# Strassen's seven quarter products for the mixing gates and merge gates of a hybrid layer

## The chip, the cores and the metric

The kernel runs on one core of a Trainium2 chip. The metric is device time in microseconds (us) of one execution. TensorE is called PE in the profile (PEld is its weight load), VectorE DVE, ScalarE ACT, GpSimd POOL and SyncE SP; SP issues nearly all DMAs.

## The reference

One decoder layer on 512 tokens of 1024 channels. The input is normalised, multiplied by one wide matrix `w_in` (1024 x 12288) and cut into pieces: `q_a, k_a, v_a, z_a` for attention, `x_m, z_m, o_m` for an mLSTM branch, and `gates`.

```python
xn = rmsnorm(h, norm_in_g[layer])
proj = xn @ w_in[layer]
q_a, k_a, v_a, z_a, x_m, z_m, o_m, gates = jnp.split(proj, SPLIT_POINTS, axis=-1)
...
y_a = (y_a * jax.nn.silu(z_a)) @ w_pa[layer]
y_m = mlstm_branch(x_m, z_m, o_m, ...) @ w_pb[layer]     # ends with h * jax.nn.silu(z_m)
g = jax.nn.sigmoid(gates.astype(jnp.float32) + gate_b[layer])
g_a, g_m = jnp.split(g, 2, axis=-1)
merged = g_a * y_a + g_m * y_m
h = h + (merged @ w_out[layer]).astype(h.dtype)
```

`z_m` has 2048 columns (the mixing gates) and `gates` has 2048 (the merge gates). Only these two projections change.

## The kernel before, in words

**Tiling.** `w_in` lies in DRAM as 96 chunks of 128 output columns, each a 128 x 1024 tile (eight blocks of 128 input channels side by side). The normalised, transposed input is held as eight pairs `xh[k]`, `xl[k]` of 128 x 512 tiles: a value is split into a rounded part (h) and the rest (l), and a product is three matmuls, h·h, h·l and l·h (`mm3`). A chunk is fetched (`fetch`, tile `raw`), split into `whi` on ACT and `wlo` on DVE (`halves`, `weights`), and multiplied by `proj_t`: 8 blocks x 3 matmuls of 512 columns into one PSUM bank. There are four buffers each of `raw`, `whi` and `wlo` (`NRAW`, `NHL`), two PSUM banks with the tag mm and six with the tag x.

**Stages.** First the sixteen `x_m` chunks with the convolution (tile `conv`), the folded q-k products (`kp`) and the S sums; this is called the xm stretch here. The S sums of a head lie in a wide tile `sraw`. Then four heads (`head`): the matmuls `num` (256 or 258 columns), their statistics on DVE, four `zm` chunks with SiLU (`silu2`), transposes `hT`, the next head's values `v` and output gate `om`, and the product `ym` with `w_pb`, summed in `ymacc`. Then eight pairs of attention heads (`qa`, `ka`, `za`, `sa`, `pT`, `pv`). Then the sixteen `gate` chunks (eight for the attention branch, tiles `thg`, and eight for the mLSTM branch, applied to `ymacc`), the product `ya` with `w_pa`, and the output projection.

**What sets the order.** All operations are recorded first. `Recorder.issue` then walks a model of the engines and gives each engine a fixed order: the ready operation of the smallest number goes first, and weights are numbered 300 earlier (`AHEAD`) so that they run ahead of their matmuls. On the chip each engine runs its list strictly in that order. Buffers come from pools of fixed size (`NSLOT` small tiles of 516 columns, `NWIDE` and `NWT` wide ones), and an operation that needs a buffer waits until one is free. Since a helper records everything, nearly all instructions carry line 333 in the profile, and one goes by the names of tiles.

Of the kernel before, what the change touches and what calls it, by code (L numbers as in the profile page):

```python
# [11 lines left out]
F32 = mybir.dt.float32  # L12
# [5 lines left out]
P = 128  # L18
T = 512
# [318 lines left out]
def hybrid_layer(ctx, tc, a, out):  # L338
# [43 lines left out]
    def mm3(ps, lh, ll, rh, rl, first, last):  # L382
        PE.matmul(ps, lh, rh, start=first, stop=False)
        PE.matmul(ps, lh, rl, start=False, stop=False)
        PE.matmul(ps, ll, rh, start=False, stop=last)
# [129 lines left out]
    for k in range(NK):  # L515
# [109 lines left out]
    def block_v(h):  # L625
# [8 lines left out]
        for s in range(NT):  # L634
# [8 lines left out]
            V.tensor_sub(v2[:, :512], ps, v1[:, :512].bitcast(F32))  # L643
            v_of[h].append((v1, v2))

    gps = pv_bank("gates")
    sps = None
    waiting = []
    sraw = []
    for ct in range(NMT):  # L650
        h, c = divmod(ct, 4)
        ps = early_ps[ct] if ct < EARLY else proj_t(CXM + ct, "xm")
        if c == 0:
            Mh, Ml = fold_qk(h)
# [19 lines left out]
        kf = slot("kf")[:, :P]  # L674
        A.activation(kf, ps[:, T - P:], AF.Copy)
        if ct == 0:
            fold_gates()
        waiting.append((ct, m, xc))
        if c == 3:

            R.together()
            for ct_, m_, xc_ in waiting:
                for i, (w, x) in enumerate(((1, m_[:, 3:259]), (1, m_[:, 259:515]), (0, xc_[:, :256]), (0, xc_[:, 256:]))):
                    PE.matmul(gps[32 * i:32 * i + 32, :256], ust[w][:, ct_, :], x, start=ct_ == 0, stop=ct_ == NMT - 1,
                              tile_position=(0, 32 * i))
# [79 lines left out]
    def head(h):  # L765
# [209 lines left out]
    for d in range(NK):
        for g in range(2):
            ps = proj_t(CG + NK * g + d, "gate")
            th = slot("thg")[:, :T]
            A.activation(th, ps, AF.Tanh, scale=0.5, bias=hs[:, 32 + 8 * g + d:33 + 8 * g + d])
            if g == 0:  # L980
                ga.append(th)
            else:
                V.scalar_tensor_tensor(ym[d], th, 1.0, ym[d], op0=OP.add, op1=OP.mult)
# [76 lines left out]
def _bucket(dist):  # L1060
# [86 lines left out]
```

## Time and profile before

| what | value |
|---|---|
| median of 3 runs | 905.69 us (904.43 to 906.78) |
| the profiled execution | 907.21 us, span 905.2 us |
| PE busy | 886.7 us, 98% of the span |
| DVE busy | 576.0 us, 64% |
| ACT busy | 385.8 us, 43% |
| POOL busy | 71.5 us, 8% |
| DMA | 104.64 MB, mean 116 GB/s |

The span is the time between the first and the last instruction of the profiled execution; the rest of its time lies around it. A busy time is the share in which at least one instruction of the engine ran. The duration of a matmul in the profile covers its whole way through the array, and the next one starts before it ends, so the cost of a matmul is read from the distance between starts.

### The profile page before, as it was taken

The page shows a single profiled execution, that of the slowest core. Times are in us where ns is not written, and L with a number is a line of the kernel's source. Part 1 is how long each engine was busy: PE and PEld are TensorE (multiplying, and loading weights), DVE is VectorE, ACT ScalarE, POOL GpSimd, SP SyncE. Part 2 cuts the span into 40 slices and gives each one's busy share as a digit, 9 for nine tenths or more (in the row PEclk, how much of TensorE's full clock was granted, in tenths as well). Part 3 has the DMA queues.
Part 4 walks back from the last instruction along what each step waited for, and adds up shares of the span by engine and source line. Part 5 has one row for each costly group of instructions (what it writes and reads, how often), then busy time and mean ns, then how long its engine had stood idle before and what let it go on. Part 6 is the DMA issues. An engine that isn't in the chain of part 4 may idle for free.

```text
span 905.2 us, 11844 instructions
## 1 busy us (share of the span) xinstructions
PE 886.7 (98%) x4340; PEld 727.1 (80%) x4340; DVE 576.0 (64%) x1154; ACT 385.8 (43%) x724; POOL 71.5 (8%) x136
## 2 busy tenths in 40 slices
PE   7899999999999999999999999999999999999997
PEld 5577878788878888887888888888888888888886
DVE  4998987785428546744855477874777843328533
ACT  7445544443343332332333265563665543325222
POOL 0950110000000000000000111101011100000000
PEclk9799999999999999999999999999999999999999
DMA  9652334233049234204313222313223223224221
GB/s 305 223 173 99 124 118 161 82 129 105 11 152 341 102 117 163 93 23 162 126 53 124 96 73 105 128 59 104 74 79 105 71 81 101 98 94 157 77 81 59
DMA packets 38801, 104.64 MB, mean 116 GB/s; under 512 B 4308, under 2 KB 6100, under 8 KB 38744
## 3 DMA queue, kind: packets, MB, share of 16 engines
q1 hardware_dynamic: 38600, 103.63, 33.6%
q8 instruction: 34, 0.56, 0.2%
q10 hardware_dynamic: 144, 0.26, 0.1%
q14 instruction: 23, 0.19, 0.1%
HBM read 93.35 MB, written 15.77 MB: 121 GB/s over the span
## 4 chain that ended last, share of the span: by engine, by line
PE 93%; DVE 4%; issue 1%; ACT 1%; DMA 1%; SPq 0%; DVEq 0%; ACTq 0%
PE zm L333 10%; PE gate L333 10%; PE ym L333 10%; PE om L333 9%; PE xm L333 8%; PE out L333 5%; PE qa L333 5%; PE za L333 5%; PE ka L333 5%; PE va L333 5%; PE ya L333 5%; PE num L333 3%; PE S L333 3%; PE pv L333 2%; PE sa L333 2%; PE pT L333 2%
## 5 line engine op out<-in xcount | busy, mean ns | idle before, releaser
L333 DVE TENSOR_TENSOR wlo<-raw,whi 128x1024 fp32r<-128x1024 f32 (+1 forms) x126 | 151.4, 1203 | 159.7 <-ACT whi L333 159.7
L333 ACT ACTIVATE whi<-raw 128x1024 fp32r<-128x1024 f32 (+1 forms) x126 | 128.1, 1019 | 284.7 <-PE zm L333 79.2
L333 PE MATMUL xm<-xh,whi 128*128 128x512 f32 x128 | 54.3, 427 | 5.2 <-ACT whi L333 5.2
L333 PE MATMUL xm<-xl,whi 128*128 128x512 f32 x128 | 54.0, 423 | 2.1 <-DVE xl L333 2.1
L333 PE MATMUL xm<-xh,wlo 128*128 128x512 f32 x128 | 53.2, 418 | 1.7 <-DVE wlo L333 1.7
L333 PE MATMUL om<-wlo,xh 128*128 128x512 f32 x128 | 50.9, 397 | 0.0
L333 PE MATMUL gate<-xh,whi 128*128 128x512 f32 x128 | 50.9, 397 | 0.0
L333 PE MATMUL zm<-xh,whi 128*128 128x512 f32 x128 | 50.8, 397 | 0.0
L333 PE MATMUL gate<-xl,whi 128*128 128x512 f32 x128 | 50.7, 396 | 0.0
L333 PE MATMUL om<-whi,xh 128*128 128x512 f32 x128 | 50.6, 396 | 0.0
L333 PE MATMUL om<-whi,xl 128*128 128x512 f32 x128 | 50.6, 395 | 0.0
L333 PE MATMUL gate<-xh,wlo 128*128 128x512 f32 x128 | 50.6, 395 | 0.0
L333 PE MATMUL ym<-yl,whi 128*128 128x512 f32 x128 | 50.5, 394 | 0.0
L333 PE MATMUL zm<-xl,whi 128*128 128x512 f32 x128 | 50.4, 394 | 0.0
L333 PE MATMUL ym<-yh,wlo 128*128 128x512 f32 x128 | 50.4, 394 | 0.0
L333 PE MATMUL zm<-xh,wlo 128*128 128x512 f32 x128 | 50.4, 394 | 0.0
L333 PE MATMUL ym<-yh,whi 128*128 128x512 f32 x128 | 50.2, 392 | 0.0
L333 ACT ACTIVATE p<-p,mx 128x128 f32<-128x128 f32 (+1 forms) x64 | 35.4, 556 | 14.3 <-DVE mx L333 14.3
L333 DVE CUSTOM_DVE_ANT_0 p<-sa,tb 128x128 f32<-128x128 f32 (+1 forms) x64 | 28.3, 488 | 18.2 <-PE sa L333 18.2
L333 DVE SCALAR_TENSOR_TENSOR conv<-xm,half,conv 128x512 f32<-128x512 f32 x48 | 37.2, 775 | 0.8
L333 DVE TENSOR_TENSOR ymacc<-ymacc,ym 128x512 f32<-128x512 f32 x24 | 16.5, 687 | 31.2 <-PE ym L333 31.2
L333 PEld LDWEIGHTS xm<-xh,whi 128*128 128x128 f32 x128 | 25.8, 201 | 11.6 <-ACT whi L333 5.8
(253 smaller groups left out, 2222.5 us busy)
## 6 DMA issues: line engine op xcount, KB each, us to landing
raw<-in_win_dram SPq DMA_DIRECT2D x94, 512.0 KB, 3.4
raw<-in_wpb_dram SPq DMA_DIRECT2D x16, 512.0 KB, 3.2
fr<-fd SPq DMA_DIRECT2D x1, 5120.0 KB
xmd<-xm SPq DMA_DIRECT2D x16, 256.0 KB, 2.2
sxd<-sx SPq DMA_DIRECT2D x16, 256.0 KB, 2.1
xmr<-xmd SPq DMA_DIRECT2D x16, 256.0 KB, 4.2
sxr<-sxd SPq DMA_DIRECT2D x16, 256.0 KB, 4.1
tb<-fr SPq DMA_DIRECT2D x16, 256.0 KB, 3.7
```

The source lines that it names most:

```text
L333: getattr(getattr(self.nc, op.eng), fn)(*a, **k)
```

## The change

Two neighbouring chunks are taken as one product of a 256 x 1024 matrix with the 1024 x 512 input, and that is cut into quarters: halves of the 1024 input channels, halves of the 512 tokens, and the two chunks. Winograd's form of Strassen's algorithm computes the four result quarters from seven products of quarters (`pair_t`) in place of eight. Each product is four blocks x 3 matmuls of 256 columns.

- The four sums and differences of the input (t1 to t4) are made once, by `quarters`, after the twelfth `x_m` chunk: POOL scales `xt` by the gain (8 operations) and forms the differences in tiles `tq` (8 operations of 512 columns), and ACT and DVE split them into `th` and `tl`.
- The four sums and differences of a pair's weights (s1 to s4) are formed by POOL in two buffers `ws` (`NWS`), and split like a chunk. A pair takes all four `whi` and `wlo` buffers: the first chunk whole (a11, a12), s2 with s1, s3 with s4, and a22 alone (`pair_weights`).
- The seven products use three PSUM banks, `ba`, `bb` and `bd`. Some of them add onto a bank that already holds another product, and DVE or ACT reads the bank between them: p1 (ACT, from ba), p1's second half and c2 (DVE, from bb), p5 (DVE, from bd).
- `xt` and the `th`, `tl` tiles share a new pool of eight tiles of 1024 columns. To make room, `NSLOT` goes from 51 to 44, `NWIDE` and `NWT` from 4 to 2, and the S sums of each head go to DRAM (`srd`) and come back in `head`.

```diff
-        z = [silu2(proj_t(CZM + 4 * h + c, "zm"), "zm") for c in range(4)]
+        z = []
+        for c in (0, 2):
+            z += silu_pair(a["win"][CZM + 4 * h + c], a["win"][CZM + 4 * h + c + 1], "zm")
...
-    for d in range(NK):
+    for d in range(0, NK, 2):
         for g in range(2):
-            ps = proj_t(CG + NK * g + d, "gate")
+            c1, c2 = pair_t(a["win"][CG + NK * g + d], a["win"][CG + NK * g + d + 1], "gate")
...
+    def quarters():
+        for k in range(NK):
+            G.tensor_scalar(xt[k], xt[k], gain(k), None, op0=OP.mult)
...
+        for m in range(2):
+            u, w = x4[m], x4[m + 2]
+            t = [slot("tq")[:, :T].rearrange("p (k t) -> p k t", k=2) for _ in range(4)]
+            G.tensor_sub(t[0], u[:, :, late], u[:, :, early])
+            G.tensor_sub(t[1], w[:, :, late], t[0])
+            G.tensor_sub(t[2], w[:, :, late], u[:, :, late])
+            G.tensor_sub(t[3], w[:, :, early], t[1])
...
+                A.activation(h[:, cc], x, AF.Copy)
+                V.tensor_sub(l[:, cc], x, h[:, cc].bitcast(F32))
...
+    def pair_weights(src0, src1):
+
+        R.ahead = AHEAD
+        r0, r1 = fetch(src0), fetch(src1)
+        lo, hi = slice(0, 512), slice(512, 1024)
+        whole = halves(r0)
...
+        G.tensor_add(s[0], r1[:, lo], r1[:, hi])
+        G.tensor_sub(s[1], s[0], r0[:, lo])
+        t2 = two(s[1], s[0])
+        s += [tile_of(wpool, [P, 512], F32, "ws", "ws", NWS) for _ in range(2)]
+        G.tensor_sub(s[2], r0[:, lo], r1[:, lo])
+        G.tensor_sub(s[3], r0[:, hi], s[1])
+        t3 = two(s[2], s[3])
+        t4 = two(r1[:, hi], None)
...
+    def pair_t(src0, src1, name):
+
+        w = pair_weights(src0, src1)
+        t1, t2, t3, t4 = tx
+        ba, bb, bd = mm_bank(name)[:, :256], sc_bank(name)[:, :256], mm_bank(name)[:, :256]
...
+        product(ba, w["a11"], x_quarter(0, 0), True)
+        A.activation(p1[:, :256], ba, AF.Copy)
+        product(bb, w["s2"], t2, True)
+        V.tensor_add(p1[:, 256:], bb, p1[:, :256])
+        product(bd, w["s1"], t1, True)
+        V.tensor_add(p5[:, :256], bd, p1[:, :256])
+        product(ba, w["a12"], x_quarter(1, 0), False)
+        product(bb, w["s3"], t3, False)
+        V.tensor_add(c2[:, 256:], bb, p5[:, :256])
+        product(bd, w["s4"], x_quarter(1, 1), False)
+        V.tensor_add(p5[:, 256:], bd, p1[:, 256:])
+        product(bb, w["a22"], t4, False)
+        V.tensor_add(c2[:, :256], bb, p1[:, :256])
...
-            sraw.append(sr)
+            SP.dma_start(srd[h], sr)
+        if ct == 11:
+            tx = quarters()
...
-        sr = sraw[h]
+        sr = wide("sraw")
+        SP.dma_start(sr, srd[h])
...
-NSLOT = 51
+NSLOT = 44
...
-NWIDE = 4
-NWT = 4
+NWIDE = 2
+NWT = 2
+NWS = 2
```

On DVE in the gate stretch (near the end of the program), a few chunks in the middle of it read so before; `wlo` is the split of a chunk, `ymacc` and `yal` are later work:

```order
L333 TENSOR_TENSOR wlo_6919<-raw_6765,whi_6909 128x1024
L333 TENSOR_TENSOR wlo_6952<-raw_6819,whi_6942 128x1024
L333 SCALAR_TENSOR_TENSOR ymacc_2370<-thg_6949,ymacc_2370 128x512
L333 TENSOR_TENSOR yal_6965<-ya_5926,yah_6900 128x512
L333 TENSOR_TENSOR wlo_6990<-raw_6856,whi_6980 128x1024
```

After the change one pair reads so, from the split of s3 of one pair to that of s3 of the next; `gate_...` are the PSUM banks, `ws` what POOL made:

```order
L333 TENSOR_TENSOR wlo_7870<-ws_7840,whi_7857 128x512
L333 TENSOR_TENSOR wlo_7877<-raw_7642,whi_7866 128x512
L333 TENSOR_TENSOR c2_7836<-gate_7753,p1_7756 128x256
L333 SCALAR_TENSOR_TENSOR ymacc_2587<-thg_7896,ymacc_2587 128x512
L333 TENSOR_TENSOR wlo_7870<-ws_7881,whi_7857 128x512
L333 TENSOR_TENSOR p1_7888<-gate_7884,p1_7888 128x256
L333 TENSOR_TENSOR p5_7931<-gate_7910,p1_7888 128x256
L333 TENSOR_TENSOR wlo_7941<-raw_7761,whi_7928 128x1024
L333 TENSOR_TENSOR wlo_7956<-ws_7925,whi_7946 128x512
L333 TENSOR_TENSOR wlo_7956<-ws_7902,whi_7946 128x512
L333 TENSOR_TENSOR c2_7971<-gate_7884,p5_7931 128x256
L333 TENSOR_TENSOR p5_7931<-gate_7910,p1_7888 128x256
```

The splits of the next pair (7941 and twice 7956) stand between p5, which follows product 3, and c2, which follows product 5 of the running pair.

On PE, at the same place, product 7 (a22, weights 7866) follows product 6 (s4, weights 7857); 7884 is bank bb and 7910 bank bd:

```order
L333 MATMUL gate_7910<-xh_471,whi_7857 128x256
L333 MATMUL gate_7910<-xl_480,whi_7857 128x256
L333 MATMUL gate_7910<-xh_471,wlo_7870 128x256
L333 MATMUL gate_7884<-th_1400,whi_7866 128x256
L333 MATMUL gate_7884<-tl_1435,whi_7866 128x256
L333 MATMUL gate_7884<-th_1400,wlo_7877 128x256
```

Product 7 writes the bank that c2_7971 on DVE reads after product 5. Before, each chunk had a bank of its own and PE had no such order to keep.

On POOL in the xm stretch, this piece of the difference shows where the scaling of `xt` and the differences `tq` stand; `ust`, `M` and `Bv` are small preparations of the heads:

```order
-L333 TENSOR_TENSOR ust<-ust,wrep 128x16x8 x7
+L333 TENSOR_TENSOR ust<-ust,wrep 128x16x8 x5
+L333 TENSOR_SCALAR xt<-xt,pc 128x512
+L333 TENSOR_TENSOR ust<-ust,wrep 128x16x8
+L333 TENSOR_SCALAR xt<-xt,pc 128x512
+L333 TENSOR_TENSOR ust<-ust,wrep 128x16x8
+L333 TENSOR_SCALAR xt<-xt,pc 128x512 x6
 L333 TENSOR_TENSOR M<-mrow,bmask 128x512 x2
 L333 TENSOR_TENSOR Bv<-brow,bmask 128x512
```

The eight scalings stand between the last of `ust` and the preparation of the second head (`M`); the eight `tq` operations follow behind `Bv`.

## Rows read from the trace of the kernel before

**Rows 1.** The page: busy time and the chain that ended last.

```profile
PE 886.7 (98%) x4340; PEld 727.1 (80%) x4340; DVE 576.0 (64%) x1154; ACT 385.8 (43%) x724; POOL 71.5 (8%) x136
...
PE 93%; DVE 4%; issue 1%; ACT 1%; DMA 1%; SPq 0%; DVEq 0%; ACTq 0%
PE zm L333 10%; PE gate L333 10%; PE ym L333 10%; PE om L333 9%; PE xm L333 8%; PE out L333 5%; PE qa L333 5%; PE za L333 5%; PE ka L333 5%; PE va L333 5%; PE ya L333 5%; PE num L333 3%; PE S L333 3%; PE pv L333 2%; PE sa L333 2%; PE pT L333 2%
```

**Rows 2.** Chain in order of time: start, us, what.

```profile
189.79 7.14 PE num L333 x60
...
196.94 22.29 PE zm L333 x96
...
728.48 81.04 PE gate L333 x349
```

**Rows 3.** Waits of PE: total, times, longest (us).

```profile
PE kp L333 <- ACT xch L333: 2.3, 2, 1.9
```

**Rows 4.** Timeline of PE in the first head's num.

```profile
192.94 0.28 PE L333 MATMUL num<-vl,Wh 128*128 128x258 f32 x1
192.95 0.19 PEld L333 LDWEIGHTS num<-vh,Wl 128*128 128x128 f32 x1
...
193.06 0.28 PE L333 MATMUL num<-vh,Wl 128*128 128x258 f32 x1
```

**Rows 5.** Timeline of POOL: start, us, instruction.

```profile
26.84 13.06 POOL L333 TENSOR_TENSOR xt<-xt,norm 128x512 f32<-128x512 f32 x8 [0.77 <-DMA wrep<-in_wrep_dram]
...
195.94 1.05 POOL L333 TENSOR_TENSOR Bv<-brow,bmask 128x512 f32<-128x512 f32 x1 [15.15 <-PE num L333]
```

**Rows 6.** Timeline of DVE beside POOL's xt work.

```profile
26.80 1.89 DVE L333 TENSOR_TENSOR xm<-xm,norm 128x512 f32<-128x512 f32 x3 [1.66 <-ACT norm L333]
...
30.89 1.75 DVE L333 SCALAR_TENSOR_TENSOR xl<-xt,pc,xh 128x512 fp32r<-128x512 f32 x1
...
32.56 2.29 DVE L333 TENSOR_TENSOR wlo<-raw,whi 128x1024 fp32r<-128x1024 f32 x1
```

**Rows 7.** Timeline of DVE in the second head.

```profile
280.08 0.42 DVE L333 SCALAR_TENSOR_TENSOR tho<-tho,num 128x256 f32<-128x256 f32 x1 [0.28 <-PE num L333]
280.42 0.17 DVE L333 BATCH_NORM_AGGREGATE mv<-bs 128x2 f32<-128x6 f32 x1
...
283.54 1.23 DVE L333 TENSOR_TENSOR wlo<-raw,whi 128x1024 fp32r<-128x1024 f32 x1
284.68 0.16 DVE L333 TENSOR_SCALAR va<-va 128x4 f32<-128x4 f32 x1
284.75 0.68 DVE L333 SCALAR_TENSOR_TENSOR zm<-zm 128x512 f32<-128x512 f32 x1
285.35 0.16 DVE L333 TENSOR_SCALAR rh_y<-va 128x4 int32<-128x4 int32 x1
```

**Rows 8.** Groups by line and form: busy, mean ns, idle before.

```profile
L333 ACT ACTIVATE whi<-raw 128x1024 fp32r<-128x1024 f32 x118 | 125.1, 1061 | 284.3 <-PE zm L333 79.2 <-PE ym L333 57.5 <-PE gate L333 50.5
...
L333 POOL CAST ql<-ql 64x512 fp32r<-64x512 f32 x16 | 9.8, 613 | 5.8 <-DVE ql L333 5.8
```

**Rows 9.** Stretches xm, ym, num and zm, gate: length, busy PE, PEld, DVE, ACT, POOL.

```profile
60.00:170.00 110.00, 109.68 (x625) 87.59 (x624) 93.15 (x144) 52.31 (x101) 7.77 (x7) 0.99 0.36 127
327.00:349.40 22.40, 22.40 (x98) 17.87 (x96) 10.87 (x13) 5.33 (x6) 1.05 (x1) 1.00 0.49 170
349.40:379.00 29.60, 29.60 (x158) 25.27 (x158) 22.14 (x64) 9.55 (x20) 0.61 (x7) 1.00 0.39 131
728.00:809.00 81.00, 81.00 (x353) 65.58 (x352) 26.96 (x30) 26.61 (x35) 0.00 (x0) 1.00 0.28 96
```

**Rows 10.** DMA issues: count, KB, us to landing.

```profile
raw<-in_win_dram SPq DMA_DIRECT2D x94, 512.0 KB, 3.4
...
xmr<-xmd SPq DMA_DIRECT2D x16, 256.0 KB, 4.2
```

More of the change, by code (lines that the diff above doesn't have):

```diff
@@ L380, in dram, with mm3 @@
         return R.buf(lambda: dpool.tile(shape, F32, name=name), shape, F32, dram=True)
[L382 to L385, printed above, removed]
+    def mm3(ps, lh, ll, rh, rl, first, last, **kw):
+        PE.matmul(ps, lh, rh, start=first, stop=False, **kw)
+        PE.matmul(ps, lh, rl, start=False, stop=False, **kw)
+        PE.matmul(ps, ll, rh, start=False, stop=last, **kw)
     def rsqrt(v, n, name):
@@ L410, in fetch, with tx_tile @@
         return raw
+    def tx_tile(name, dt=F32R):
+        return tile_of(upool, [P, 1024], dt, name, "tx", 8)
     def halves(raw):
@@ L431, in hybrid_layer @@
     EARLY = 4
-    pair = [wide("xt") for _ in range(NK // 2)]
+    pair = [tx_tile("xt", F32)[:, :] for _ in range(NK // 2)]
     xt = [pair[k // 2][:, k % 2 * T:k % 2 * T + T] for k in range(NK)]
@@ L520, in hybrid_layer @@
     R.ahead = 0
+    def quarters():
+        for k in range(NK):
+            G.tensor_scalar(xt[k], xt[k], gain(k), None, op0=OP.mult)
+        x4 = [q.rearrange("p (k t) -> p k t", k=2) for q in pair]
+        early, late = slice(0, T // 2), slice(T // 2, T)
+        forms = []
+        for m in range(2):
[5 more added lines that the diff above has]
+            G.tensor_sub(t[3], w[:, :, early], t[1])
+            forms.append(t)
+        out = []
+        for i in range(4):
+            h, l = tx_tile("th"), tx_tile("tl")
+            for m in range(2):
+                cc = slice(m * T, m * T + T)
+                x = forms[m][i].rearrange("p k t -> p (k t)")
+                A.activation(h[:, cc], x, AF.Copy)
+                V.tensor_sub(l[:, cc], x, h[:, cc].bitcast(F32))
+            out.append([(h[:, k * 256:k * 256 + 256], l[:, k * 256:k * 256 + 256]) for k in range(NK // 2)])
+        return out
@@ new lines, in x_quarter, with two @@
+    def x_quarter(r, c):
+        cc = slice(256 * c, 256 * c + 256)
+        return [(xh[k][:, cc], xl[k][:, cc]) for k in range(4 * r, 4 * r + 4)]
+    def pair_weights(src0, src1):
[3 more added lines that the diff above has]
+        whole = halves(r0)
+        def two(x, y):
+            h = tile_of(wpool, [P, 1024], F32R, "whi", "whi", NHL)
+            l = tile_of(wpool, [P, 1024], F32R, "wlo", "wlo", NHL)
+            for cc, z in ((lo, x), (hi, y)):
+                if z is not None:
+                    A.activation(h[:, cc], z, AF.Copy)
+                    V.tensor_sub(l[:, cc], z, h[:, cc].bitcast(F32))
+            return h, l
+        s = [tile_of(wpool, [P, 512], F32, "ws", "ws", NWS) for _ in range(2)]
+        G.tensor_add(s[0], r1[:, lo], r1[:, hi])
[6 more added lines that the diff above has]
+        t4 = two(r1[:, hi], None)
+        R.ahead = 0
+        cut = lambda w, c: (w[0][:, c], w[1][:, c])
+        return dict(a11=cut(whole, lo), a12=cut(whole, hi), s2=cut(t2, lo), s1=cut(t2, hi),
+                    s3=cut(t3, lo), s4=cut(t3, hi), a22=cut(t4, lo))
@@ new lines, in pair_t, with product @@
+    def pair_t(src0, src1, name):
+        w = pair_weights(src0, src1)
+        t1, t2, t3, t4 = tx
+        ba, bb, bd = mm_bank(name)[:, :256], sc_bank(name)[:, :256], mm_bank(name)[:, :256]
+        def product(ps, a, b, first):
+            kw = {} if first else {"skip_group_check": True}
+            for k in range(4):
+                cc = slice(k * P, k * P + P)
+                mm3(ps, a[0][:, cc], a[1][:, cc], b[k][0], b[k][1], first and k == 0, k == 3, **kw)
+        p1 = slot("p1")[:, :512]
+        p5 = slot("p5")[:, :512]
+        c2 = slot("c2")[:, :512]
+        product(ba, w["a11"], x_quarter(0, 0), True)
[11 more added lines that the diff above has]
+        V.tensor_add(c2[:, :256], bb, p1[:, :256])
+        return (ba, p5[:, 256:]), c2
@@ L522, in proj_t, with silu_pair @@
+    def silu_pair(src0, src1, name):
+        c1, c2 = pair_t(src0, src1, name)
+        z0 = slot(name)[:, :T]
+        for i in range(2):
+            h = z0[:, 256 * i:256 * i + 256]
+            A.activation(h, c1[i], AF.Tanh, scale=0.5)
+            V.scalar_tensor_tensor(h, h, 1.0, c1[i], op0=OP.add, op1=OP.mult)
+        return [z0, silu2(c2, name)]
     def proj_t(chunk, name):
@@ L648, in hybrid_layer @@
     waiting = []
-    sraw = []
     for ct in range(NMT):
@@ L974, in hybrid_layer @@
     ga = []
[L975 removed]
+    for d in range(0, NK, 2):
         for g in range(2):
[L977 to L979 removed]
+            c1, c2 = pair_t(a["win"][CG + NK * g + d], a["win"][CG + NK * g + d + 1], "gate")
+            bias = [hs[:, 32 + 8 * g + d + c:33 + 8 * g + d + c] for c in range(2)]
+            th = slot("thg")[:, :T], slot("thg")[:, :T]
+            A.activation(th[0][:, :256], c1[0], AF.Tanh, scale=0.5, bias=bias[0])
+            A.activation(th[0][:, 256:], c1[1], AF.Tanh, scale=0.5, bias=bias[0])
+            A.activation(th[1], c2, AF.Tanh, scale=0.5, bias=bias[1])
             if g == 0:
[L981 removed]
+                ga += th
             else:
[L983 removed]
+                for c in range(2):
+                    V.scalar_tensor_tensor(ym[d + c], th[c], 1.0, ym[d + c], op0=OP.add, op1=OP.mult)
     go = const("go", [P, D], F32)
```

7 lines of the change are left out of this document (3 added, 4 removed).

## The prediction, made before the changed kernel was run

> **What bounds the kernel now.** I read the share of busy time first, then the chain that ended last, then the waits of PE, then the stretches around the two places that the change rewrites. PE is busy 98% of the span and carries 93% of the chain; the two projections that change, zm and gate, are 10% of it each [rows 1]. In time order the chain is solid PE from 181 us to 897 us: each run of 96 or 349 matmuls follows the one before without a hole [rows 2], and the largest wait of PE behind the start-up is 2.3 us in two pieces, for an activation copy [rows 3]. So PE time saved in zm and gate is saved time, as long as nothing new makes PE wait. The second thing to see is how much room DVE has: 27.0 of 81 us in the gate stretch, but 22.1 of 29.6 us in a head's num and zm stretch and 93.2 of 110 us in the xm stretch [rows 9].
>
> **The change, part by part.**
>
> *PE work removed.* A pair of chunks costs 48 matmuls of 512 columns now. They start 0.2322 us apart (22.29 us over 96, and 81.04 over 349) [rows 2], so 11.15 us a pair. The change makes it 84 matmuls of 256 columns. The num stage already runs matmuls of 256 and 258 columns with a new weight load for each: 60 in 7.14 us, 0.119 us apart [rows 2], with the loads beside them [rows 4]. 84 of these are 10.0 us. That is 1.15 us less a pair, and 18.4 us for the 16 pairs; at the spacing of the single rows (0.12 us) it would be 17.1. I take 18.1. Against the change stands one rule: the Trainium skill, "TensorE: Matmul & The Clock Gate", Part 3, "The mechanism", says that a weight load overlaps running matmuls only where it goes to another group of rows; each load here fills the whole array. By that rule 576 more loads would be paid in full, and Strassen would lose. The rows of num disagree: loads of 0.19 us stand inside a spacing of 0.12 us. What it would cost is a rival below.
>
> *The prepared activations (quarters).* 16 more POOL operations and 8 more splits on ACT and DVE, in the xm stretch. A POOL operation on 128x512 with two SBUF inputs takes 1.05 us alone [rows 5]; the eight that scale xt by one operand have no row, and lie between 0.61 (a cast of one input) [rows 8] and 1.05 us. POOL has the time. DVE is the one that pays: while POOL worked on xt (eight in 13.06 us), DVE operations with two SBUF inputs took 1.05 to 1.1 us longer each (wlo 2.29 us, xl 1.76 us), while three xm operations with one input in PSUM ran at 0.63 us each beside the same POOL work [rows 5, 6, 7]. So a POOL operation and a two-SBUF-input DVE operation exclude each other. The DVE price is 8 x 0.60 = 4.8 us of splits (0.60 us is the spacing of 512 columns back to back) [rows 7] plus at most 16 x 1.05 = 16.8 us of blocking, against 16.9 us in which DVE is idle between 60 and 170 us [rows 9]. Between 0 and 21.6 us could reach PE; PE has other chunks to multiply there, and it absorbed the blocking by the first xt work with few waits [rows 3], so I take 3 us.
>
> *The weights of a pair.* Before, a pair was two DVE subtractions of 1024 columns (1.14 us apart) [rows 7]. Now it is one of 1024, five of 512 and five PSUM adds of 256 columns (0.34 us apart): 1.14 + 5 x 0.60 + 5 x 0.34 = 5.84 us against 2.28, with 4 POOL operations (4.2 us) beside it. ACT goes from two copies of 1.06 us [rows 8] to one and five shorter ones, in stretches where it is a third busy [rows 9]. In a head, one SiLU in two halves adds 0.08 us a pair on DVE (2 x 0.34 against 0.60).
>
> *The new wait.* Products 2, 5 and 7 share one PSUM bank (bb), and 3 and 6, and 1 and 4, share one each. Product 5 must wait until p1 has read bb, product 7 until c2 has read it. From the end of product 3 to the start of product 7 there are three products, 3 x 12 x 0.119 = 4.28 us. In that time ACT and DVE have in this order: the copy of the next pair's first weights (1.06; its buffer is freed by product 3), the subtraction (1.14), two of 512 (0.60 each), then c2 (0.34): 3.74 us, and some 0.3 us of matmul drain and handing over (a 256-column matmul lasts 0.28 us at 0.12 spacing [rows 4]). Slack about 0.2 us. Behind a late c2 stand product 7 and all that follows on PE.
>
> *Gate stretch, 8 pairs.* Followed with these durations, a pair whose POOL operations fall on PSUM adds or idle DVE has no stall; a pair that follows a merge-gate pair has two ymacc updates more, meets one POOL operation (up to 1.05 us), and c2 comes about 0.3 us late. That is 0.15 us a pair, 1.2 in all; bounds 0 and 8 x 0.8 = 6.7 us (a whole blocking less the slack). The first pair is laced into the last attention heads, where until now matmuls without any DVE dependence filled PE: 1 us more. Together 2.2 us.
>
> *Heads, 4 x 2 pairs.* In the num and zm stretch DVE would have 22.1 + 2 x (5.84 + 0.08 - 2.28) = 29.4 us of work in 29.6 - 2.3 = 27.3 us. The weights of the first pair (4.1 us of it) are made before num, in the ym stretch, where DVE is busy 10.9 of 22.4 us [rows 9]; that leaves 25.3, and two POOL operations that meet DVE bring 2.1: 27.4. DVE is just full, and PE waits on p1 and c2 now. I take 1 us a head, 4 us; bounds 0 and 6.3 us a head (2.1 over and four blockings).
>
> *The trip of the S sums through DRAM.* Four stores and four loads of 640 KB; loads of 256 and 512 KB land in 4.2 and 3.4 us [rows 10], and each load stands in SP's queue well ahead of its head. Nothing; if a load came late it would cost its landing, 4 to 5 us once. *Fewer slots and wide tiles:* PE's order through attention stays row for row until the last two heads, so nothing there.
>
> Sum, against the profiled execution of 907.2 us: -18.1 + 3 + 2.2 + 4 = -8.9, so 898.3. Runs without the profile have their median 1.5 us lower: 896.8, I say 897 us.
>
> **The rivals.** *Nearly all of the gain lands:* planned slack hides the DVE work as it hid the xt work, stalls at most 3 us; 888 to 892 us. For it: PE has almost no waits now. Chance 0.12.
>
> *DVE becomes the bound in the heads as well as the gates:* c2 and p1 late in each pair by most of what a pair saves. Gate pairs with all POOL work serial to DVE take 5.84 + 0.60 (ymacc) + 4.2 = 10.6 us against 10.0 on PE, and heads lose 2 to 3 us each; with 3 us in the xm stretch the time is 903 to 908 us. Chance 0.14; it covers "no change".
>
> *Slower:* one mechanism, the bank adds in the heads. If the first pair's weights are not made ahead of num, DVE is 2.1 us over and each blocking by POOL comes on top: 6.3 us a head, 25 us in all, against 18.1: 905.7 + 7 + 5 for the other two terms = 918 at the end of it, 909 to 912 in the milder half. It decides from about 3.2 us a head on (18.1 less 5.2 of the other terms, over four). For it: DVE is 75% busy there, and its order puts next weights ahead of c2. Against it: the ym stretch before is half idle on DVE. Chance 0.12.
>
> *Loads in the open:* 576 more loads of 0.19 us would add 108 us: 997 us. The rows of num speak flatly against it. Chance 0.01.
>
> **How the numbers follow.** My forecast, 892 to 903 us, has 0.61. The range 888 to 908 leaves out the slow rival, the loads and the best of the good one, about 0.17. 0.3% is 2.7 us, about what a measurement of this kernel can tell from no change: faster means under 903.0, slower over 908.4. Faster 0.61 + 0.12 = 0.73, same 0.14, slower 0.13.
>
> **What would show it.** In the changed profile matmuls of zm and gate with 256 columns should start 0.119 us apart inside a product; if they don't, the first term is wrong. PE's waits should name DVE (p1 and c2, that is, zm and gate matmuls waiting for DVE) with some 0.15 us a pair in the gates and 1 us a head; DVE subtractions beside ws operations should be about 1 us longer than their 0.69 us, PSUM adds should not be. In the xm stretch, waits of PE on xch, kph or xl of some 3 us. The forecast is wrong if these waits sum to under 4 or over 15 us, or if PE waits for raw or sraw loads.

## The result: 1.6% slower

The changed kernel takes 919.44 us (median of 4 runs, 917.78 to 923.88) against 905.48 us (904.43 to 906.78) for the kernel before in the same job: ratio 1.0161, 95% interval 1.0122 to 1.0200. The forecast was 897 us, with a range up to 908. The medians are 14.0 us apart; the profiled execution has a span of 916.9 us where the kernel before had 905.2, 11.7 more, and what follows divides up these 11.7. Its page, busy time and the chain that ended last [rows 1]:

```profile
PE 876.1 (96%) x4916; PEld 742.1 (81%) x4916; DVE 670.1 (73%) x1314; ACT 428.1 (47%) x828; POOL 190.8 (21%) x216
...
PE 65%; DVE 8%; issue 4%; ACT 3%; POOL 3%; DMA 2%; POOLq 0%; DVEq 0%; ACTq 0%; SPq 0%
PE om L333 8%; PE ym L333 7%; PE zm L333 6%; PE out L333 5%; PE qa L333 5%; PE va L333 5%; PE ka L333 5%; PE za L333 5%; PE ya L333 5%; PE num L333 3%; DVE wlo L333 3%; POOL ws L333 3%; PE pv L333 2%; PE sa L333 2%; PE pT L333 2%
```

PE is busy 10.6 us less, and its share of the chain fell from 93% to 65%: the end now hangs on DVE, ACT and POOL too, on `wlo` and `ws` above all. The waits of PE that are new or grew [rows 3]:

```profile
PE zm L333 <- DVE p L333: 4.6, 4, 1.5
PE gate L333 <- DVE c L333: 4.2, 7, 1.5
PE kp L333 <- DVE xcl L333: 3.7, 2, 3.5
...
PE num L333 <- ACT Wh L333: 2.5, 2, 1.2
...
PE S L333 <- DVE kpl L333: 1.3, 2, 0.8
PE zm L333 <- DVE c L333: 1.2, 1, 1.2
```

The six listed come to 17.5 us. They lie in three stretches: the xm stretch ahead of the first num (called the front below), the heads, and the gates. This table has the start of the first matmul of four stages, from the timelines of PE (us), of the two kernels and of all runs below. Where marked *, products of zm run ahead of num or among it, so that only the later columns compare. The four columns come from one profiled execution of each kernel and the ratio from all its runs; a profiled execution lies up to 4.2 us from the median of its kernel (e15; 2.7 in e4).

| kernel | num | va | gate | out | ratio to before (95%) |
|---|---|---|---|---|---|
| before | 189.6 | 460.6 | 715.0 | 853.9 | |
| changed | 197.2 | 474.0 | 728.7 | 864.9 | 1.0161 (1.0122, 1.0200) |
| e1 no weight sums | 194.7 | 463.5 | 718.5 | 848.3 | 0.9961 (0.9945, 0.9976) |
| e2 weight sums on DVE | 195.4 | 468.9 | 723.4 | 855.2 | 1.0039 (1.0024, 1.0054) |
| e3 banks and order | 195.8 | 472.0 | 727.7 | 863.6 | 1.0130 (1.0110, 1.0150) |
| e4 no quarters | 188.2 | 465.6 | 720.3 | 856.0 | 1.0064 (1.0040, 1.0089) |
| e5 all sums off POOL | 186.3* | 465.2 | 719.8 | 851.2 | 0.9989 (0.9980, 0.9999) |
| e6 gates alone | 188.1 | 461.2 | 718.1 | 849.8 | 0.9970 (0.9960, 0.9981) |
| e7 buffers alone | 190.2 | 464.9 | 720.2 | 859.0 | 1.0060 (1.0042, 1.0079) |
| e8 idle sums on POOL | 189.5 | 460.5 | 714.9 | 858.8 | one run, 912.19 us |
| e9 buffers, fr paced | 190.3 | 460.8 | 717.6 | 856.4 | 1.0023 (1.0013, 1.0033) |
| e10 changed, fr paced | 196.9 | 475.3 | 731.1 | 867.4 | 1.0145 (1.0128, 1.0162) |
| e11 e5, fr paced | 194.8* | 464.5 | 719.8 | 851.3 | 0.9959 (0.9943, 0.9974) |
| e12 e6, fr paced | 188.2 | 458.8 | 716.1 | 847.6 | 0.9934 (0.9919, 0.9949) |
| e13 no POOL work, fr paced | 188.1 | 452.8 | 708.1 | 837.8 | 0.9852 (0.9835, 0.9870) |
| e14 e11, another bank | 195.5* | 458.5 | 713.6 | 845.9 | 0.9904 (0.9885, 0.9923) |
| e15 quarters on DVE | 197.3 | 478.7 | 735.4 | 871.4 | 1.0137 (1.0110, 1.0164) |

Of the changed kernel against before: the front is 7.6 us longer, the heads (num to va) 276.8 in place of 271.0 us, attention 254.7 for 254.4, gate and ya (to out) 136.2 for 138.9. Eight pairs in the heads and eight in the gates were to save 9.2 us each, so the heads lost 15.0 us and the gates 6.5. Sum: 7.6 + 5.8 + 0.3 - 2.7 = 11.0 us, where the spans differ by 11.7.

What a late pair looks like, in the gate stretch: timeline of the changed kernel, start and us (PE's rows of the product before and of product 7 alone):

```profile
762.03 1.29 POOL L333 TENSOR_TENSOR ws<-ws,raw 128x512 f32<-128x512 f32 x1 [1.61 <-issue]
762.15 2.24 DVE L333 TENSOR_TENSOR wlo<-raw,whi 128x1024 fp32r<-128x1024 f32 x1
...
763.35 1.15 ACT L333 ACTIVATE whi<-ws 128x512 fp32r<-128x512 f32 x2 [2.03 <-POOL ws L333]
...
764.14 0.28 PE L333 MATMUL gate<-xl,whi 128*128 128x256 f32 x1
764.25 0.28 PE L333 MATMUL gate<-xh,wlo 128*128 128x256 f32 x1
...
764.32 1.28 DVE L333 TENSOR_TENSOR wlo<-ws,whi 128x512 fp32r<-128x512 f32 x2
...
765.53 0.41 DVE L333 TENSOR_TENSOR c<-gate,p 128x256 f32<-128x256 f32 x1
765.75 1.28 POOL L333 TENSOR_TENSOR ws<-raw 128x512 f32<-128x512 f32 x1 [2.43 <-DVE wlo L333]
...
765.99 0.39 PE L333 MATMUL gate<-th,whi 128*128 128x256 f32 x1 [1.46 <-DVE c L333]
```

POOL starts 0.12 us ahead of the 1024-column `wlo`, which then takes 2.24 us for 1.23 [rows 7]. The two splits of 512 columns and c2 stand behind it on DVE, and product 7, which shares c2's bank, starts 1.5 us late. POOL in turn waits for a `ws` buffer that DVE frees. Seven c2 are late in the gates, and six of them stand behind such a `wlo`, of 1.63 to 2.24 us.

In the heads the operations that POOL holds up are often tiny ones. Here, in the third head, two statistics of 4 columns that take 1.25 and 1.00 us stand ahead of the p that PE waits for; the row at 383.19 has the usual length of such an operation. Beside the first POOL makes a weight sum, beside the second `Bv`, which the kernel before has too:

```profile
379.95 1.66 POOL L333 TENSOR_TENSOR ws<-raw,ws 128x512 f32<-128x512 f32 x1 [2.75 <-DVE wlo L333]
380.39 1.25 DVE L333 TENSOR_SCALAR rh_t<-rh_t 128x4 f32<-128x4 f32 x1
...
382.16 1.00 DVE L333 TENSOR_TENSOR rh_y<-rh_y,rh_t 128x4 f32<-128x4 f32 x1
383.19 0.16 DVE L333 TENSOR_TENSOR rh_y<-rh_y,rr 128x4 f32<-128x4 f32 x1
...
385.83 0.42 DVE L333 TENSOR_TENSOR p<-zm,p 128x256 f32<-128x256 f32 x1
...
386.30 0.58 PE L333 MATMUL zm<-th,whi 128*128 128x256 f32 x1 [1.52 <-DVE p L333]
```

Counted over the trace of the changed kernel, DVE operations that last over 0.4 us longer than the median of their kind are 15 in the heads (13.3 us more in all) and 14 from gate to out (11.4 us more). The kernel before and e1 below have none in either place.

The groups of POOL in the changed kernel (busy, mean ns):

```profile
L333 POOL TENSOR_TENSOR ws<-raw 128x512 f32<-128x512 f32 x32 | 43.7, 1367 | 182.6 <-DMA raw<-in_win_dram 69.5 <-DVE wlo L333 56.3 <-DVE rh_y L333 23.8
L333 POOL TENSOR_TENSOR ws<-raw,ws 128x512 f32<-128x512 f32 x16 | 23.7, 1480 | 40.3 <-DVE wlo L333 40.3
L333 POOL TENSOR_TENSOR ws<-ws,raw 128x512 f32<-128x512 f32 x16 | 22.4, 1400 | 8.2 <-POOL ws L333 4.8 <-issue 2.9
L333 POOL TENSOR_SCALAR xt<-xt,pc 128x512 f32<-128x512 f32 x8 | 15.4, 1934 | 0.0
```

### The profile page after: what moved, and what is told of

The parts are those of the page before. It is cut to its first block, busy times and chain, and to the rows that moved or that the text cites. A ratio compares the mean times of both kernels' runs of the same rounds, so it can differ in the third digit from the quotient of the medians.

```text
span 916.9 us, 13507 instructions
## 1 busy us (share of the span) xinstructions
PE 876.1 (96%) x4916; PEld 742.1 (81%) x4916; DVE 670.1 (73%) x1314; ACT 428.1 (47%) x828; POOL 190.8 (21%) x216
## 4 chain that ended last, share of the span: by engine, by line
PE 65%; DVE 8%; issue 4%; ACT 3%; POOL 3%; DMA 2%; POOLq 0%; DVEq 0%; ACTq 0%; SPq 0%
PE om L333 8%; PE ym L333 7%; PE zm L333 6%; PE out L333 5%; PE qa L333 5%; PE va L333 5%; PE ka L333 5%; PE za L333 5%; PE ya L333 5%; PE num L333 3%; DVE wlo L333 3%; POOL ws L333 3%; PE pv L333 2%; PE sa L333 2%; PE pT L333 2%
## 5 line engine op out<-in xcount | busy, mean ns | idle before, releaser
L333 ACT ACTIVATE whi<-raw 128x1024 fp32r<-128x1024 f32 (+1 forms) x126 | 121.0, 963 | 153.5 <-PE zm L333 30.0
L333 POOL TENSOR_TENSOR ws<-raw 128x512 f32<-128x512 f32 x32 | 43.7, 1367 | 182.6 <-DMA raw<-in_win_dram 69.5
L333 ACT ACTIVATE whi<-ws 128x512 fp32r<-128x512 f32 x64 | 38.6, 627 | 52.8 <-POOL ws L333 25.7
L333 DVE TENSOR_TENSOR wlo<-ws,whi 128x512 fp32r<-128x512 f32 x64 | 46.9, 753 | 12.5 <-ACT whi L333 11.7
L333 PE MATMUL zm<-th,whi 128*128 128x256 f32 x128 | 37.3, 292 | 5.9 <-DVE p L333 4.0
L333 PE MATMUL gate<-th,whi 128*128 128x256 f32 x128 | 36.9, 289 | 4.2 <-DVE c L333 4.2
L333 PE MATMUL zm<-tl,whi 128*128 128x256 f32 x128 | 36.5, 285 | 0.0
L333 PE MATMUL zm<-th,wlo 128*128 128x256 f32 x128 | 36.4, 286 | 0.0
```

The source lines that it names most:

```text
L333: getattr(getattr(self.nc, op.eng), fn)(*a, **k)
```

## Experiments

Theory A was: POOL's sums shut DVE out, so `wlo`, p1, c2 and `xcl` come late. Rivals were B (the shared PSUM banks), C (DVE's own added work), D (the smaller pools) and, from e7 on, E (transfers).

**e1, no weight sums.**

```diff
...
-        G.tensor_add(s[0], r1[:, lo], r1[:, hi])
-        G.tensor_sub(s[1], s[0], r0[:, lo])
-        t2 = two(s[1], s[0])
+        t2 = two(r1[:, lo], r1[:, hi])
...
-        G.tensor_sub(s[2], r0[:, lo], r1[:, lo])
-        G.tensor_sub(s[3], r0[:, hi], s[1])
-        t3 = two(s[2], s[3])
+        t3 = two(r1[:, lo], r1[:, hi])
```

> The changed kernel without the four POOL operations that form a pair's weight sums (64 of them): ACT and DVE split plain quarters of the second weight chunk instead, so their work and PE's is the same and only POOL's is left out, and the values with it. Theory A (a POOL operation of 1.3 us shuts DVE out, so wlo, p1, c2 and E come late): the heads keep about 4 us of their 15 lost, the gate stretch about 1 of 6: 919.4 - 11 - 5 = 903, 900 to 907. Rival B (the shared PSUM banks make products 5 and 7 wait whatever POOL does): 916 to 920. Rival C (DVE's own added work is too much): 911 to 916, with zm and gate still waiting for DVE by 8 us or more.

Measured 903.62 us. From gate to out 129.8 us: 9.1 less than before, the whole gain of the gates. In the heads 268.8 us: 8.0 came back, 7.0 did not. So POOL's sums are what costs in the gates and about half of what costs in the heads; B and C fall in the gates. In e1 nobody waits for POOL's results either, so by itself it can't tell A from sums that are merely ready too late; the lengthened DVE operations counted above and e8 speak for A.

**e2, the weight sums on DVE** (`G` becomes `V` in the same four lines).

> The changed kernel with the four weight sums of a pair on DVE in place of POOL. DVE gets 4 x 0.6 = 2.4 us more work a pair, and loses the 4 x 1.3 us in which POOL shuts it out. Theory A (blocking by POOL): faster than the changed kernel, 905 to 914, the gate pairs at 10.0 to 10.2 us. Rival B (shared banks): 916 to 921. Rival C (DVE's own work is the bound): slower than the changed kernel, 922 to 930.

Measured 910.15 us. DVE has 44 us more work of its own, and the kernel is faster by 1.2%. The three groups of sums (means of 686, 685 and 685 ns):

```profile
L333 DVE TENSOR_TENSOR ws<-raw 128x512 f32<-128x512 f32 x32 | 21.9, 686 | 3.0 <-DMA raw<-in_win_dram 2.8
L333 DVE TENSOR_TENSOR ws<-raw,ws 128x512 f32<-128x512 f32 x16 | 11.0, 685 | 0.2
L333 DVE TENSOR_TENSOR ws<-ws,raw 128x512 f32<-128x512 f32 x16 | 11.0, 685 | 0.1
```

A sum costs DVE 0.69 us if it makes it; if POOL does, a DVE operation beside it can last up to 1.1 us longer (1.25 for 0.17 above). C's forecast (slower) is refuted.

**e3, banks and order.** Product 2 gets a bank of its own, and product 5 moves ahead of product 4.

```diff
-        ba, bb, bd = mm_bank(name)[:, :256], sc_bank(name)[:, :256], mm_bank(name)[:, :256]
+        ba, b2, bd = mm_bank(name)[:, :256], sc_bank(name)[:, :256], mm_bank(name)[:, :256]
+        bb = sc_bank(name)[:, :256]
...
-        product(bb, w["s2"], t2, True)
-        V.tensor_add(p1[:, 256:], bb, p1[:, :256])
+        product(b2, w["s2"], t2, True)
+        V.tensor_add(p1[:, 256:], b2, p1[:, :256])
...
+        product(bb, w["s3"], t3, True)
+        V.tensor_add(c2[:, 256:], bb, p5[:, :256])
         product(ba, w["a12"], x_quarter(1, 0), False)
-        product(bb, w["s3"], t3, False)
-        V.tensor_add(c2[:, 256:], bb, p5[:, :256])
...
```

> The changed kernel with product 2 in a PSUM bank of its own and the products in the order 1 2 3 5 4 6 7, so that product 5 waits for no bank and products 6 and 7 have two products (2.8 us) in which the sum they wait for can be read, in place of one. POOL and DVE do as many operations as before. Rival B (shared banks): the waits for p and c go, some 10 us: 907 to 911. Theory A (POOL shuts DVE out, DVE is behind by more than a product): part of the gate stretch's waits go, the heads keep theirs: 914 to 918.

Measured 918.35 us: by the intervals no different from the changed kernel. The gate stretch is 135.9 us. PE still waits 4.2 us for p in zm and 1.3 for c in the gates, where slack of two products replaced one. B falls as the main cause.

**e4, no quarters.**

```diff
-            tx = quarters()
+            tx = [x_quarter(r, c) for r in range(2) for c in range(2)]
```

> The changed kernel without the quarters of the activations: plain quarters of xh and xl are multiplied, so 24 POOL operations and 16 splits in the xm stretch are left out, and the values are not the reference's. Theory A (the quarters' POOL work shuts DVE out there): the first num starts at 189 to 191 us as before the change, 911 to 913 in all. Rival D (the smaller pools cost the 7 us in front): 917 to 920. If only the 3 us that were predicted come from the quarters: 915 to 917.

Measured 912.85 us, and the first num at 188.2, 9.0 us ahead of the changed kernel. Not all of it is the quarters': at their 160th matmul the two executions are already 1.1 us apart (55.0 and 53.9 us), before the first operation of the quarters (55.5 us). So the quarters cost some 7.9 us in front, not 3; the medians differ by 6.6. That D explains the front is refuted. (The quarters are 16 operations of POOL; the 24 of the expectation is a slip, here and in e13.)

**e15, the quarters on DVE.** This run came last, to tell A from the quarters' own work.

```diff
-            G.tensor_scalar(xt[k], xt[k], gain(k), None, op0=OP.mult)
+            A.activation(xt[k], xt[k], AF.Copy, scale=gain(k))
...
-            G.tensor_sub(t[0], u[:, :, late], u[:, :, early])
+            V.tensor_sub(t[0], u[:, :, late], u[:, :, early])
...
```

> The changed kernel with the quarters at the same place, their scaling on ACT and their sums on DVE (8 more DVE operations of 0.69 us, none on POOL). If POOL's exclusion is what the quarters cost: first num at 189 to 192 us against 197.2, 5 to 8 us under the changed kernel, 911 to 914. If it is the quarters' own work on a DVE that is full there: 197 to 201, and the changed kernel's time or more, 919 to 923.

Measured 920.72 us, num at 197.3 (its profiled execution is the longest of its four, so its later columns say little). **Theory A's forecast fell here:** without one POOL operation in them the quarters cost as much. That doesn't clear POOL in the changed kernel. There PE's wait stands directly behind four DVE operations beside POOL's work, `conv`, `tl`, `sx` and `xcl`, which together last 4.2 us longer than the same four a little earlier or later (0.68, 0.68, 0.48 and 0.69 us); timeline (start, us):

```profile
133.16 1.77 DVE L333 SCALAR_TENSOR_TENSOR conv<-cth,conv 128x512 f32<-128x512 f32 x1
134.34 1.74 POOL L333 TENSOR_TENSOR tq<-xt,tq 128x512 f32<-128x512 f32 x1
134.85 1.79 DVE L333 TENSOR_TENSOR tl<-tq,th 128x512 fp32r<-128x512 f32 x1
136.06 3.10 POOL L333 TENSOR_TENSOR tq<-xt 128x512 f32<-128x512 f32 x2
136.56 1.48 DVE L333 TENSOR_SCALAR sx<-conv,hs 128x512 f32<-128x512 f32 x1
137.97 1.74 DVE L333 TENSOR_TENSOR xcl<-conv,xch 128x512 fp32r<-128x512 f32 x1
...
139.76 0.52 PE L333 MATMUL kp<-xcl,Mh 128*128 128x512 f32 x1 [3.45 <-DVE xcl L333]
```

In e15 the waits moved:

```profile
PE kp L333 <- ACT xch L333: 5.9, 2, 4.0
...
PE xm L333 <- ACT xm L333: 2.5, 1, 2.5
```

And e15 isn't free of POOL in this stretch: two weight sums stand there at 147.8 and 149.7 us, and of the six `conv` beside them two last 1.0 us longer each, ahead of the wait of 4.0. No run keeps all POOL sums out of the xm stretch and leaves the quarters in it, so how much of the 7.9 us is exclusion and how much DVE's and ACT's added work stays open. The stretch has no room for this work, by whichever engine. In e5, where the same ACT and DVE work stands in om instead, the first num starts at 186.3, but PE then waits for it inside num.

**e5, all sums off POOL**: e2, e3 and e15 together, with the quarters called behind head 0's om.

```diff
-        if ct == 11:
-            tx = quarters()
...
         if h == 0:
             gate_o(h)
+            tx.extend(quarters())
```

> The whole change with all its POOL sums moved: weight sums on DVE, product 2 in a bank of its own and the order 1 2 3 5 4 6 7, and the quarters made in the om stretch of head 0 (the scaling on ACT, the sums on DVE) instead of the xm stretch. Against the kernel before: theory A (what was lost was POOL's blocking, in three places): the first num where it was before (within 2 us), the heads 3 to 7 us shorter, the gate stretch 7 to 9 us shorter, in all 9 to 15 us faster, ratio 0.984 to 0.990. If DVE's own added work is what fills the heads (rival C): the heads gain nothing and the ratio is 0.991 to 0.996.

Measured 905.92 us, 0.1% under before: the gates gain 7.5 us, and front and heads together end 4.6 us later than before. It misses both ranges. PE waits 3.4 us for `tho` in head 0, 3.1 us for p at om, and 2.1 us (0.8 for `wlo`, 1.3 for `whi`) for om weights in the second head. The first of these stands behind the quarters' own splits on DVE, so the quarters aren't free in om either:

```profile
192.66 3.69 DVE L333 TENSOR_TENSOR tl<-tq,th 128x512 fp32r<-128x512 f32 x6
...
198.48 0.39 PE L333 MATMUL num<-vh,Wh 128*128 128x256 f32 x1 [3.44 <-DVE tho L333]
```

**e6, Strassen in the gates alone** (the four lines of zm as before, the quarters made in attention).

> Strassen in the merge gates alone, zm as before the change; weight sums on DVE, the product order and banks of the run with the split banks, the quarters made in the attention stretch by ACT and DVE, where DVE is busy 150 of 210 us. Theory A: the gate stretch is 7 to 9 us shorter, the attention stretch 0 to 3 longer, everything ahead as before: 5 to 9 us faster than the kernel before, ratio 0.990 to 0.995. If the smaller pools cost something (rival D): less by that.

Measured 904.92 us: gates 131.7 for 138.9, attention 256.9 for 254.4, and 2.3 us of PE waiting for `xmr` in the second head. That is 2.4 us faster than its kernel before, outside A's range; D's "less by that" fits, as e7 and e12 show.

**e7, the buffers alone.**

```diff
-NSLOT = 51
+NSLOT = 44
...
-            sraw.append(sr)
+            SP.dma_start(srd[h], sr)
```

> The kernel before with the change's buffers alone: 44 slots for 51, two wide tiles of each kind for four, the S sums' trip through DRAM, xt in the new tiles. No Strassen. The prediction: nothing, within 1 us of the kernel before. Rival D (the buffers cost the front or the heads): 3 to 7 us slower.

Measured 912.07 us, 4.8 us slower: D holds for the kernel before, and the 0 of the prediction was wrong there. The heads take 3.7 us longer, and the place is the second head; SP's queue there in the kernel before, then in e7, then PE's wait in e7:

```profile
279.46 6.16 SPq L333 DMA_DIRECT2D xmr<-xmd  x4
```

```profile
291.03 7.49 SPq L333 DMA_DIRECT2D raw<-in_wpb_dram  x3
298.84 0.97 SPq L333 DMA_DIRECT2D xmr<-xmd  x2
```

```profile
PE v L333 <- DMA xmr<-xmd: 2.3, 1, 2.3
```

`xmr` is issued 19 us later, behind loads of S sums and `sxr` and behind the write of `fr` (16 heads of 128x640, 5.2 MB, issued at 274.7 us), which keeps the DMA engines full for over 20 us.

**e9 to e12, the write of fr paced.**

```diff
-        SP.dma_start(fr, fd[:, None, :].to_broadcast([16, P, 640]))
...
+    def spread_bias(p, mark):
+        hold, R.hold = R.hold, (*R.hold, mark)
+        for hd in (2 * p, 2 * p + 1):
+            SP.dma_start(fr[hd], fd[:, None, :].to_broadcast([16, P, 640])[hd])
+        R.hold = hold
```

e9, e7 with the pacing:

> The run with the change's buffers alone, and the one 5.2 MB write of the relative biases (fr), which stands in the second head's stretch, cut into its 16 heads and issued two at a time through the attention stretch. If that burst and the S sums' loads meet (rival E, the transfers): the second head's wait for xmr is gone, and the time is within 1.5 us of the kernel before. If the missing slots themselves are what costs: 4 to 5 us above it, as without the pacing.

Measured 909.01 us, 2.8 us above its kernel before: outside both forecasts, nearer to E's. The heads are as before (270.5 us), attention 2.4 longer; whether by the paced write itself or by the missing slots isn't separated.

e10, the changed kernel with it:

> The changed kernel with the write of fr paced in the same way and nothing else. Rival E: the second head is 2 to 4 us shorter, the rest as in the changed kernel: 8 to 10 us above the kernel before. If the transfers cost the changed kernel nothing: 11.5 to 14 above it, as it was.

Measured 919.89 us: ratio 1.0145, no different from the changed kernel. E costs the changed kernel nothing that can be measured; that the transfers hide there behind what DVE is late by anyway is my reading and not shown.

e11, e5 with it and the quarters earlier:

> The run with all the sums moved off POOL, the write of fr paced, and the quarters one step earlier in program order, ahead of head 0's work. POOL and the transfers together: the second head has no wait for weights, the wait of head 0's num for tho (3.4 us) goes, 6 to 10 us faster than the kernel before, ratio 0.989 to 0.993. If DVE's own work fills the heads: no more than 3 us faster.

Measured 902.62 us, ratio 0.9959: between the two forecasts. It changes two things (pacing, and the place of the quarters), so e5 against e11 doesn't separate them. PE now waits 5.4 us for p at the step from zm to om (3.1 in e5), and no longer 3.4 for `tho`.

e12, e6 with it:

> Strassen in the gates alone, with the write of fr paced. Rival E: the second head's wait for xmr (2.5 us) goes: 4 to 6 us faster than the kernel before, ratio 0.993 to 0.996, and 2 to 3 us under the same kernel without pacing.

Measured 900.60 us, ratio 0.9934, as E had it; the wait for `xmr` is gone. By the ratios e12 is 0.36%, 3.3 us, under e6, a little more than the 2 to 3 forecast.

**e13, none of the change's POOL work, fr paced** (e1, e4 and the pacing).

> The changed kernel without the 64 POOL weight sums, without the quarters (24 POOL operations, 16 splits), and with the write of fr paced: PE's work is that of the change, DVE keeps its splits and bank adds; plain quarters stand in for the sums, and the values are not the reference's. If POOL's exclusion and the transfers are all that was lost, the predicted PE saving of 18 us lands: 888 to 892, ratio 0.980 to 0.984. If DVE's own added work fills the heads: 5 to 8 us of waits stay there, 894 to 898.

Measured 893.32 us, ratio 0.9852, between the two forecasts. Gate to out takes 129.7 us (9.2 less), the heads 264.7 (6.3 less). Of the remaining 2.9 us of the heads 2.3 are waits, 1.5 for `xmr` and 0.8 for c. So the PE term was right in the gates, and DVE's own splits and bank adds cost no more than 2.9 us in the heads.

**e14, another bank.** e11 with `bd` from the ring of six banks in place of the ring of two.

```diff
-        ba, b2, bd = mm_bank(name)[:, :256], sc_bank(name)[:, :256], mm_bank(name)[:, :256]
+        ba, b2, bd = mm_bank(name)[:, :256], sc_bank(name)[:, :256], sc_bank(name)[:, :256]
```

> The run with all sums moved off POOL and the write of fr paced, with the bank of products 3 and 6 taken from the six-bank ring in place of the two-bank ring mm, so that om's first bank doesn't wait for p5. If the ring is what holds the step from zm to om: the 5.4 us of om waiting for p go, 896 to 899. If DVE is simply behind there: the wait moves to hT or tho and the time stays at 901 to 904.

Measured 898.29 us, ratio 0.9904: 0.55% under e11. The wait of om for p is gone; what PE waits for `tho` is 0.8 us in all, for `xmr` 2.7. This version computes all that the reference has and beats both kernels.

**e8, idle sums on POOL**, the disputed cost by itself, in the kernel before.

```diff
+            for _ in range(2):
+                G.tensor_add(slot("ws")[:, :512], raw[:, :512], raw[:, 512:])
```

> The kernel before with 32 POOL sums of 128x512 in the gate stretch, two a chunk, whose results nobody reads. PE and DVE have as much work as before, DVE with 54 us idle of 81. Theory A: the time stays (905 to 908), and a 128x1024 wlo beside two of the POOL sums lasts 2.2 us or more in place of 1.14 to 1.22; without exclusion it stays at 1.2 and the POOL sums alone get longer. POOL's sum of two plain raw halves: 1.3 us, not the 1.05 of the rows for Bv.

Measured 912.19 us, where about 907 was expected. Nobody waits for these sums, so they can't cost by coming late. The loss isn't where DVE is half idle (from 734 us on PE has no wait), but at 716 to 724 us, where PE falls some 4.9 us behind the kernel before and sums fell beside the last softmaxes. In e8:

```profile
713.10 10.14 POOL L333 TENSOR_TENSOR ws<-raw 128x512 f32<-128x512 f32 x7
...
716.21 3.21 DVE L333 TENSOR_SCALAR p<-p,sm 128x128 f32<-128x128 f32 x3
```

The same three instructions in the kernel before:

```profile
716.28 0.88 DVE L333 TENSOR_SCALAR p<-p,sm 128x128 f32<-128x128 f32 x3
```

In the groups of e8 from 715 to 809 us a POOL sum took 1.65 us on average, and `wlo` of 1024 columns 1.42, not the 2.2 expected. Who pays depends on who starts first. In the gates of the changed kernel the sums that started 0.12 to 0.74 us ahead of a 1024-column `wlo` lasted 1.28 to 1.29 us and the `wlo` 1.63 to 2.24; in e8 the sums that started 0.24 to 1.02 us after the start of one lasted 2.27 to 2.28 us themselves.

## Why the prediction was wrong

The saving on PE was sized rightly. What failed are the three prices of waiting, 3 us for the quarters, 2.2 for the gates and 4 for the heads: measured in the profile they are 7.9, 6.5 and 15.0, 29.4 us in place of 9.2.

**The PE term was right.** Matmuls of a product start 0.11 to 0.12 us apart (rows of 764 us above), and e13's gates save 9.2 us where eight pairs at 1.13 to 1.15 were forecast. The loads-in-the-open rival is out.

**"A POOL operation on 128x512 with two SBUF inputs takes 1.05 us alone" was mis-sized.** That row [rows 5] is `Bv`, whose operands are broadcast. A sum of plain halves takes 1.28 to 1.29 us (timeline above), and 1.40 on average over the 64 in the changed kernel.

**"So a POOL operation and a two-SBUF-input DVE operation exclude each other" was too narrow.** DVE operations with one SBUF tensor and scalars are shut out too: `sx` took 1.48 us at 136.56, a statistic of 4 columns 1.25 at 380.39, and in e8 `p<-p,sm` 3.21 us for three in place of 0.88. The Trainium skill, "SBUF — State Buffer", section "SBUF: two separate sides", states the lock for DVE operations in a two-port mode as well as for those with two SBUF inputs; these rows agree. The half of that rule that I hadn't weighed is the one that would reach `sx` and the scalings of the softmax; in which mode they ran no row shows. Bank adds were not shut out, as predicted: 0.41 us each beside POOL.

**The gates, "0.15 us a pair, 1.2 in all" and 1 us for the first pair, were 6.5 us.** The mechanism was as put (c2 late at product 7), and the loss reached the forecast's bound (given as 6.7; 8 x 0.8 is 6.4); I chose the value near the other end. e1 shows that it is POOL's sums almost entirely (6.4 of the 6.5 us come back), e2 that DVE can make them itself at 2.1 us (131.8 against 129.7).

**The heads, "I take 1 us a head, 4 us", were 15.0 us**, 3.75 a head. That is past the slower rival's point of decision of 3.2, but its condition wasn't met: in three of the four heads all splits of the first pair's weight sums stand on DVE 4.6 to 15 us ahead of num, and in the first head half of them do. What the sum had wrong is the count of blockings, two a head: 3, 3, 5 and 4 DVE operations a head last over 0.4 us longer, 13.3 us in all, seven of them the small statistics. e1 puts 8.0 us of the 15.0 to POOL's sums. Of the 7.0 that e1 leaves, 4.1 went in e13, which differs by the quarters and the pacing of fr; e1's trace names the transfers (timelines of ACT, DVE and PE):

```profile
301.51 1.06 ACT L333 ACTIVATE whi<-raw 128x1024 fp32r<-128x1024 f32 x1 [5.52 <-DMA raw<-in_win_dram]
```

```profile
302.60 1.22 DVE L333 TENSOR_TENSOR wlo<-raw,whi 128x1024 fp32r<-128x1024 f32 x1 [4.40 <-ACT whi L333]
303.74 0.54 DVE L333 TENSOR_SCALAR tho<-tho,mv,rh_y 128x512 f32<-128x512 f32 x1
```

```profile
304.34 0.90 PE L333 MATMUL hT<-ident,tho 128*128 128x128 f32 x3 [4.21 <-DVE tho L333]
```

ACT waited 5.5 us for raw weights (loads landed after 15.1 us in the median there, 3.4 in [rows 10]), DVE's `wlo` for ACT, and behind it on DVE stood the `tho` on which PE waited 4.2 us; from 304.3 to 307.7 us the granted clock was then 0.50. How the 15.0 divides in the changed kernel itself, where POOL and transfers overlap (e10), stays open.

**The quarters, "I take 3 us", were some 7.9** (6.6 by the medians). That PE "absorbed the blocking by the first xt work with few waits" was no evidence for this stretch: DVE was busy 93 of 110 us there, and PE's operations that need `xcl` and `xch` keep their order. The blocking on which I based the price is there, 5.9 us on six DVE operations between 133 and 145 us, and the 3.45 us of waiting stand behind four of them. A cost that the sum didn't have came behind it: PE was busy 0.31 of 3.70 us up to 139.7, and the granted clock was 0.55 on average over the next 3.8. e15 shows that the same work on ACT and DVE costs as much there; whether ACT or DVE is first to be late I didn't separate.

**The S sums' trip through DRAM, "Nothing", and fewer slots and wide tiles, "nothing there",** was wrong for the kernel before (4.8 us, e7) and harmless in the changed one (e10). I looked at PE's order and at landing times of 3 to 4 us, and not at the 5.2 MB write in the second head, beside which such loads land.

## What to carry to other kernels

An elementwise sum that goes to POOL to relieve DVE can cost DVE more than it saves: here up to 1.1 us of exclusion against 0.69 us for making it, and operations of 4 columns pay it as well as those of 1024. Where PE saves little per unit (1.15 us a pair), first look for the stretch where the extra operand work is cheapest (the quarters cost some 8 us in xm, at least 3.4 us of waiting in om, and 1.6 in attention, where e6 is compared with e7), and only then move it between engines. A buffer that shrinks moves transfers in the queue; look for the largest burst there, not for the mean landing time.

## What the runs showed of the hardware

After a stretch with long waits PE ran one product at the lower of its two clock levels. Windows of the changed kernel (length, then busy PE, PEld, DVE, ACT, POOL, granted clock, DMA share, GB/s):

```profile
383.00:386.20 3.20, 1.29 (x8) 0.74 (x6) 3.13 (x9) 1.61 (x3) 0.14 (x1) 0.95 0.81 303
386.20:389.20 3.00, 2.90 (x14) 2.90 (x14) 2.64 (x4) 0.00 (x0) 0.00 (x0) 0.50 0.24 67
389.20:392.00 2.80, 2.80 (x26) 2.80 (x24) 1.32 (x4) 1.24 (x2) 0.00 (x0) 0.99 0.84 285
```

PE was busy 1.29 of 3.20 us, and then 0.50 was granted (1.2 GHz): twelve matmuls of zm, from 386.30 to 389.09 us, took 2.8 us where 1.4 is usual. The wait of 1.5 us for p so cost about 1.4 more.
